# Raw weight sums behind a product's subtraction, softmax kept out of the sigmoid pairs, and a pinned gating, in a hybrid decoder step

## The chip, the cores and the metric

The kernel runs on one core of a Trainium2 chip. The core has a matrix engine (TensorE, PE in the profile), three engines for elementwise work (VectorE or DVE, ScalarE or ACT, GpSimd or POOL), a queue engine that here only issues transfers (SyncE or SP), and 16 DMA engines. Each engine works through its own list of instructions in order; an instruction that waits holds up all that stand behind it on the same engine. The metric is the device time of one execution in microseconds (us), as the median of several runs.

## The reference

One layer of a decoder with two parallel branches, stick-breaking attention and a gated short convolution, for a prompt of 512 tokens with 16 meta tokens ahead of it and for 8 sequences that each decode 4 tokens against 512 cached ones. Everything is float32.

```python
def mixer_layer(x, conv_hist, attend, g_pre, w_in, b_sb, b_gate, w_conv, b_conv, w_pa, w_pc, w_out, g_post):
    h = rmsnorm(x, g_pre)
    q, k, v, ga, cb, cc, ch, gc, ma, mc = jnp.split(h @ w_in, split_offsets(), axis=-1)
    ...
    a = attend(q, k, v, b_sb).reshape(bsz, t, D_ATTN) * jax.nn.silu(ga)
    u = cc * ch
    u_ext = jnp.concatenate([conv_hist.astype(u.dtype), u], axis=1)
    c = cb * causal_conv(u_ext, w_conv, b_conv) * jax.nn.silu(gc)
    merged = (jax.nn.sigmoid(ma + b_gate[:D_MODEL]) * (a @ w_pa)
              + jax.nn.sigmoid(mc + b_gate[D_MODEL:]) * (c @ w_pc))
    y = x + rmsnorm(merged @ w_out, g_post)
    return y, k, v, u_ext[:, -(CONV_WIDTH - 1):]
```

D_MODEL is 2048, the attention and the convolution have 1024 channels each (8 heads of 128), ma and mc 2048 each. The attention weight of a key is `sigmoid(z)` times the product of `1 - sigmoid(z)` over the keys between it and the query, computed in log space.

## The kernel before, in words

**Precision.** Every float32 operand of a large product is split in two parts, high and low, and a product is three matmuls: high x high, high x low, low x high. Weights come as raw tiles of 128 x 1024 (`w_load`, tile `raw`, one DMA each on SP's queue); `w_split` makes the high part on ACT (`whi`, L240) and the low part on DVE (`wlo`, L241). PE cannot start a product before its `whi`, nor its last third of matmuls before `wlo`.

**Seven products for eight.** For ga, cb, cc, ch, gc, ma and mc, `pair` computes two column blocks at once. It cuts the tokens into two halves and the 2048 rows of weights into two halves; that is a 2 x 2 block product, which `seven` does with seven block products in the place of eight (Strassen in Winograd's form). Each `product` is 24 matmuls (L971). The weights of the seven are `w11`, four sums and differences, `w12` and `w22`. The sums are made on DVE: `w21 + w22` (L983), that plus `w11` (L986), `w21 + w11` in place (L994), and another (L1000). L983 and L994 add raw tiles only, so they can run as soon as the DMAs have landed; both are wanted by products later in the pair. Results collect in PSUM banks: `x` and `q` from one pool (tile `mm`), `y` from another (tile `o`). In the middle of a pair, L997 subtracts a saved part from `y` to give the block (1, 1); only after that may PE write the next product into `y`. L1002 gives the block (0, 1) in the same way from `q`. The caller uses each block as it is yielded: with Silu (ga, gc), a multiplication (L1052 to L1057, L1070, L1073: the convolution) or Sigmoid on ACT (ma, mc: L1118).

**The stages.** The head of the kernel normalizes the tokens and makes q, k and v; four heads of the prompt are attended at once (`head_now`; all this takes 365 us). Then come the pairs: ga (4 pairs, tile `sg`), the convolution (4 times CC, CH, GC, CB), and the gates ma and mc (16 pairs, tile `g`). The gates are written to a scratch tensor in HBM. The pairs run from 365 to 1170 us. Then `w_pc` is applied, one group of columns at a time (L256; each group's result is multiplied with the gate `gt` read back from scratch, L1208), the four later heads are attended, and the attention outputs are multiplied by silu(ga) (`gated`, L1161). For the four early heads, both `at` and `sg` come back by DMA from scratch. At the end come `w_pa` and `w_out`.

**Decoding beside it.** `decode_steps` is a generator whose pieces are set between the products. It computes logits against the cached keys on DVE (1024 dot products, L781, each of two rows in the listings below; `kpage` and `qb` are loaded by POOL's queue), then the log-space softmax on ACT and DVE (L467 to L470 by `softplus_acts`, and L840 and L842), and then the product with the cached values (`vpage`).

**What sets the order.** Within each engine a scheduler decides it, from dependencies and from its own estimates. The kernel has two means against it. `pin`, which is `tc.keep_in_program_order`, keeps an instruction in its place relative to the other pinned ones. `tc.issue_after(ins)`, used by the change, has the instructions issued inside it come behind `ins` in the order. ACT holds one table of functions at a time; where the next function needs another, an ACT_TABLE_LOAD is inserted (Sigmoid on one side, Exp and Ln on the other). `preload_act_table_set(LNEXP)` places such a load by hand.

Of the kernel before, what the change touches and what calls it, by code (L numbers as in the profile page):

```python
# [2 lines left out]

# [57 lines left out]
def hybrid_step_kernel(  # L61
# [404 lines left out]
    def softplus_acts(e, l, r, src, bias, pin=lambda ins: ins):  # L466
        pin(act.activation(e, src, AF.Abs, bias=bias))  # L467
        pin(act.activation(e, e, AF.Exp, scale=-1.0))
        pin(act.activation(l, e, AF.Ln, bias=one_c[:e.shape[0]]))
        pin(act.activation(r, src, AF.Relu, bias=bias))  # L470

    def softplus_sums(e, l, r, t):
        dve.tensor_scalar(out=t, in0=e, scalar1=1.0, scalar2=-1.0, op0=ALU.add, op1=ALU.add)
        dve.tensor_sub(t, e, t)
        dve.tensor_add(r, r, l)
        dve.tensor_add(r, r, t)

    def softplus_parts(e, l, r, t, src, bias, pin=lambda ins: ins):

        softplus_acts(e, l, r, src, bias, pin)  # L480
        softplus_sums(e, l, r, t)


    d3ctx, hlctx, hctx, nctx = (ExitStack() for _ in range(4))
# [274 lines left out]
    def decode_steps():  # L759
# [45 lines left out]
        with tc.tile_pool(name="dec2", bufs=1, side="right") as d2:  # L805
            def tl(name, n=1):
                return d2.tile([P, n * BHT], F32, name=name)

            e, l, r, t = tl("de", 4), tl("dl", 4), tl("dr", 4), tl("dt", 4)
            S = tl("dS")  # L810
            dve.tensor_copy(S.rearrange("p (b h t) -> p b h t", b=DB, h=H),
                            bsb.unsqueeze(1).unsqueeze(3).broadcast_to([P, DB, H, DT]))
            for pg in range(NPG):
                dve.tensor_add(flat(z_all[:, pg]), flat(z_all[:, pg]), S)

            dve.memset(S, 0.0)
            rn = S[:TS]
            for p0 in (2, 0):
                pin(act.preload_act_table_set(LNEXP))
                if p0:  # L820
                    softplus_parts(e[:TS, :BHT], l[:TS, :BHT], rn, t[:TS, :BHT], zn, zero_c[:TS], pin)
                    mask_new(rn)
                c = slice(p0 * BHT, (p0 + 2) * BHT)
                softplus_parts(e[:, c], l[:, c], r[:, c], t[:, c], zf[:, c], zero_c, pin)
                if p0:
                    pn = z_ps()[:TS, :BHT]
                    pe.matmul(pn, lhsT=neg_u.bitcast(F32)[:TS, :TS], rhs=rn, start=True, stop=True)
                    dve.tensor_add(zn, pn, zn)

                for pg in (p0 + 1, p0):  # L830
                    rp = r[:, pg * BHT:(pg + 1) * BHT]
                    pz = z_ps()[:, :BHT]
                    pe.matmul(pz, lhsT=neg_u.bitcast(F32), rhs=rp, start=True, stop=False)
                    pe.matmul(pz, lhsT=neg_one.bitcast(F32), rhs=S, start=False, stop=True)
                    dve.tensor_add(flat(z_all[:, pg]), pz, flat(z_all[:, pg]))
                    if pg > 0:
                        dve.tensor_add(S, S, rp)
                yield
            pin(act.preload_act_table_set(LNEXP))
            pin(act.activation(zn, zn, AF.Exp))  # L840
            mask_new(zn)
            pin(act.activation(zf, zf, AF.Exp))  # L842
        yield "weights"

        d3 = d3ctx.enter_context(tc.tile_pool(name="dec3", bufs=1, side="right"))
# [3 lines left out]
        for g in range(2):  # L849
            for hf in range(2):  # L850
                cs = slice(hf * 512, (hf + 1) * 512)
                po = t_ps()

                def pages(vts, last):
                    for n, (lhs, rhs, pg, j) in enumerate(vts):
                        pin(pe.matmul(po[32 * j:32 * (j + 1), :], lhsT=lhs, rhs=rhs, start=(pg == 0),  # L856
                                      stop=last and n >= len(vts) - 4, tile_position=(0, 32 * j), skip_group_check=True))

                for pp in range(0, NPG, 2):
                    vts = []  # L860
                    for pg in (pp, pp + 1):
                        for j in range(4):
                            vt = d3.tile([P, 512], F32, name="vpage", bufs=9)
                            page_load(vt, vc, 4 * g + j, pg, cs)
                            vts.insert(0, (A_all[:, pg, 4 * g + j].rearrange("p h t -> p (h t)"), vt, pp, j))
                    if g + hf + pp == 0:
                        yield "values"
                    if pp == 0:
                        vts[4:] = [(l, r, 1, j) for l, r, _, j in vts[4:]]
                    else:  # L870
                        vts += [(An[:, 4 * g + j, :], vflat[:, cs], NPG, j) for j in reversed(range(4))]
                    pages(vts, pp > 0)
                    if pp == 0:
                        yield
                ob = d3.tile([P, 512], F32, name="ob")
                act.copy(ob, po)
                pt = t_ps()
                for hh in range(4):
                    pe.transpose(out=pt[:, hh * P:(hh + 1) * P], in_=ob[:, hh * P:(hh + 1) * P], identity=ident)
                for hh in range(4):  # L880
                    h = 4 * hf + hh
                    src = pt[:, hh * P:(hh + 1) * P].rearrange("p (j h t) -> p j h t", h=H, t=DT)[:, :, h, :]
                    ss = slice(16 * g, 16 * (g + 1))
                    dve.tensor_mul(sg_s[:, h, ss].rearrange("p (j t) -> p j t", t=DT), src,
                                   sg_s[:, h, ss].rearrange("p (j t) -> p j t", t=DT))
                yield

    dec = decode_steps()
    dec_at = set()
# [73 lines left out]
    def gate_bias(j, w):  # L963
        return bg[:, KD * w + j:KD * w + j + 1]

    def product(o, w, rhs, start, stop):
        hi, lo = w
        for k in range(8):
            rh, rl = rhs(k)
            for m, (l, r) in enumerate(((hi, rh), (hi, rl), (lo, rh))):  # L970
                pe.matmul(o, lhsT=l[:, k, :], rhs=r, start=(start and k == 0 and m == 0),  # L971
                          stop=(stop and k == 7 and m == 2), skip_group_check=True)

    def seven(ws, n, rb, rt, s, tmp, sums=None):

        w11, w21, w22, w12 = ws
        sums = sums or (lambda m: tmp("c"))  # L980
        x, q, y = mm_ps()[:, :n], mm_ps()[:, :n], o_ps()[:, :n]
        product(x, w_split(w11), rb(0, 0), True, False)
        dve.tensor_add(s, w21, w22)  # L983
        product(q, w_split(s), rb(0, 1), True, False)
        act.activation(y, x, AF.Copy, scale=-1.0)
        dve.tensor_add(s, s, w11)  # L986
        product(y, w_split(s), rt(0), False, False)
        s5 = tmp("s5")
        act.copy(s5, q)
        product(x, w_split(w12), rb(1, 0), False, True)  # L990
        s2 = tmp("s2")
        act.copy(s2, y)
        yield 0, 0, x
        dve.tensor_add(w21, w21, w11)  # L994
        product(y, w_split(w21), rt(1), False, False)
        c22 = sums(1)
        dve.tensor_sub(c22, y, s5)  # L997
        yield 1, 1, c22
        dve.tensor_add(s, s, w12)
        product(q, w_split(s), rb(1, 1), False, True)  # L1000
        c12 = sums(0)
        dve.tensor_sub(c12, q, s2)  # L1002
        yield 0, 1, c12
        product(y, w_split(w22), rt(2), False, True)
        yield 1, 0, y
# [28 lines left out]
    def by_query(m, half):  # L1034
        return slice(half * HQ, (half + 1) * HQ)
# [78 lines left out]
    for j in range(0, KD, 2):  # L1114
        for w, c in ((0, COL_MA), (1, COL_MC)):
            gs = [q_tile("g") for _ in range(2)]
            for m, half, b in pair(c + j * P, HQ):
                act.activation(gs[m][:, by_query(m, half)], b, AF.Sigmoid, bias=gate_bias(j + m, w))  # L1118
            if j + 2 * w == KD:
                tc.keep_in_program_order(act.preload_act_table_set(LNEXP))  # L1120
            for m in range(2):
                gate_out(j + m, w, gs[m])
            dec_group()
            if j + w == 14:

                after = hl[0].tile([P, P], F32, name="after")
                dve.tensor_scalar_add(after, neg_u.bitcast(F32), 1.0)
                loaded = head_loads(NOW, hl[0])
# [27 lines left out]
            nc.sync.dma_start(cr[:, i, :], c_scr[k + i])  # L1156
            split_evac(c_hl[:, k + i, :], c_hl[:, 8 + k + i, :], cr[:, i, :], cr[:, i, :])

    def gated(h, x, sg):

        dve.tensor_mul(sg, x, sg)  # L1161
        split_evac(a_hl[:, h, 0:PQ], a_hl[:, 8 + h, 0:PQ], sg, sg)

    def gate_load(h):
# [34 lines left out]
    for j in range(KD):  # L1199
        if j in HERE:  # L1200
            h = HERE[j]
# [12 lines left out]
        if j - 2 in HERE:  # L1214
            k = HERE[j - 2] - NOW
            sg, at = sgs.pop(k)
            gated(k, at, sg)
    split_evac(a_hl[:, 0:8, PQ:TQ], a_hl[:, 8:16, PQ:TQ], sg_s, sg_s)
    hlctx.close()
    dctx.close()  # L1220
# [51 lines left out]
    with tc.tile_pool(name="outp", bufs=1) as op:  # L1272
# [88 lines left out]
        for j in range(0, KD - 2, 2):  # L1361
# [4 lines left out]
            def tmp(name):  # L1366
                return op.tile([P, HQ], F32, name=name)
# [130 lines left out]
```

## Time and profile before

| what | value |
|---|---|
| three runs | 1580.3, 1583.6 and 1583.96 us; median 1583.6 |
| the profiled execution | 1584.74 us |
| its span, first to last instruction | 1583.1 us |
| mean granted clock of TensorE | 0.994 |
| casts `whi<-raw` / `whi<-s`, L240 | 247 and 126, 1051 and 1048 ns each |
| low parts `wlo<-raw` / `wlo<-s`, L241 | 247 and 126, 1222 and 1224 ns each |
| dot products L781 | 1024, 246.0 us of busy time |
| DMA | 252.77 MB, a mean of 160 GB/s |

The rows that follow in the text are of four kinds. A row of the page's chain gives shares of the span. A row of the view of waits reads: who waits, for whom, then the total in us, the number of waits and the longest. A row of the timeline reads: start in us from the start of the span, duration, engine, line, instruction, tile written and tiles read, sizes; in brackets at its end, how long the engine stood still ahead of it and what released it. A row of the windows gives a stretch, its length, the busy time of each engine with the number of instructions (PE, weight loads, DVE, ACT, POOL), the granted clock, the share of DMA and the GB/s.

### The profile page before, as it was taken

How to read it: one execution, taken by the hardware profiler on the slowest of the kernel's cores; microseconds unless marked ns; L12 is line 12 of the kernel's file. 1: busy time of each engine (PE TensorE's matmuls, PEld its weight loads, DVE VectorE, ACT ScalarE, POOL GpSimd, SP SyncE). 2: the span in 40 equal slices, each digit the busy share in tenths (PEclk: the TensorE clock that was granted, in tenths of full speed). 3: DMA queues.
4: the chain of work that ended last, by engine and by line, in shares of the span. 5: the costliest groups of instructions: out<-in, count | busy, mean ns of one | idle time of the engine just before them, and what ended most of it. 6: DMA issues, size and time to landing. Idle time of an engine off the chain costs nothing.

```text
span 1583.1 us, 32334 instructions
## 1 busy us (share of the span) xinstructions
PE 1560.7 (99%) x12172; PEld 1527.5 (96%) x12172; DVE 1268.5 (80%) x3574; ACT 761.7 (48%) x1345; POOL 234.7 (15%) x428
## 2 busy tenths in 40 slices
PE   8999999999999999999999999999999999999997
PEld 7999999999999999999999999898899999999997
DVE  7329999956799999999999997565678857877776
ACT  6245555435444444444444457444476734345552
POOL 1123333222111010011011102312100010000000
PEclk9999999999999999999999999999999999999999
DMA  8245556344454544445465545767595455433345
GB/s 263 82 137 186 168 160 184 107 130 136 150 180 124 151 130 140 146 134 162 120 181 173 162 138 168 245 194 226 157 306 172 148 178 165 152 107 94 101 143 183
DMA packets 300674, 252.77 MB, mean 160 GB/s; under 512 B 11521, under 2 KB 268613, under 8 KB 299701
## 3 DMA queue, kind: packets, MB, share of 16 engines
q1 hardware_dynamic: 272021, 160.45, 35.1%
q0 software_dynamic: 28368, 89.98, 17.0%
q8 instruction: 95, 1.56, 0.4%
q14 instruction: 62, 0.51, 0.1%
q10 hardware_dynamic: 128, 0.27, 0.1%
HBM read 217.95 MB, written 32.71 MB: 158 GB/s over the span
## 4 chain that ended last, share of the span: by engine, by line
PE 94%; DVE 2%; ACT 1%; DMA 1%; issue 1%; DVEq 0%; SPq 0%; ACTq 0%
PE mm L971 32%; PE mm L256 27%; PE o L971 24%; PE mm L321 2%; PE z L702 1%; PE o L714 1%; PE z L321 1%; PE tp L856 1%; DMA raw<-in_w_in 1%; PE z L620 1%; PE z L1439 1%; PE tp L505 0%; PE z L1293 0%; DVE wlo L241 0%; DMA at<-a_scr 0%
## 5 line engine op out<-in xcount | busy, mean ns | idle before, releaser
L240 ACT CAST whi<-raw 128x1024 fp32r<-128x1024 f32 x247 | 259.4, 1051 | 375.5 <-PE mm L971 135.0
L241 DVE TENSOR_TENSOR wlo<-raw,whi 128x1024 fp32r<-128x1024 f32 x247 | 301.7, 1222 | 90.2 <-ACT whi L240 88.0
L971 PE MATMUL mm<-h_hi,whi 128*128 128x272 f32 (+1 forms) x1152 | 333.5, 289 | 0.7 <-ACT whi L240 0.7
L971 PE MATMUL mm<-h_hi,wlo 128*128 128x272 f32 (+1 forms) x1152 | 332.6, 290 | 0.0
L971 PE MATMUL mm<-h_lo,whi 128*128 128x272 f32 (+1 forms) x1152 | 332.5, 289 | 0.0
L971 PE MATMUL o<-t_hi,whi 128*128 128x272 f32 (+1 forms) x864 | 251.6, 291 | 3.3 <-DVE c L997 3.3
L971 PE MATMUL o<-t_lo,whi 128*128 128x272 f32 (+1 forms) x864 | 251.2, 291 | 0.0
L971 PE MATMUL o<-t_hi,wlo 128*128 128x272 f32 (+1 forms) x864 | 251.1, 291 | 0.0
L781 DVE CUSTOM_DVE_ANT_0 junk<-kpage,qb 128x128 f32<-128x128 f32 x1024 | 246.0, 287 | 4.0 <-DMA qb<-q_scr 3.7
L971 PEld LDWEIGHTS mm<-h_hi,whi 128*128 128x128 f32 x1152 | 217.4, 189 | 6.1 <-ACT whi L240 3.5
L971 PEld LDWEIGHTS mm<-h_lo,whi 128*128 128x128 f32 x1152 | 216.8, 188 | 0.9 <-issue 0.8
L971 PEld LDWEIGHTS mm<-h_hi,wlo 128*128 128x128 f32 x1152 | 217.0, 189 | 0.2
L240 ACT CAST whi<-s 128x1024 fp32r<-128x1024 f32 x126 | 132.0, 1048 | 151.2 <-PE mm L971 48.5
L241 DVE TENSOR_TENSOR wlo<-s,whi 128x1024 fp32r<-128x1024 f32 x126 | 154.2, 1224 | 62.8 <-ACT whi L240 61.3
L256 PE MATMUL mm<-h_lo,whi 128*128 128x280 f32 (+1 forms) x640 | 187.6, 293 | 0.0
L256 PE MATMUL mm<-h_hi,wlo 128*128 128x280 f32 (+1 forms) x640 | 187.1, 293 | 0.0
L256 PE MATMUL mm<-h_hi,whi 128*128 128x280 f32 (+1 forms) x640 | 186.7, 292 | 0.0
L971 PEld LDWEIGHTS o<-t_hi,whi 128*128 128x128 f32 x864 | 164.1, 190 | 4.0 <-DVE c L997 4.0
L971 PEld LDWEIGHTS o<-t_hi,wlo 128*128 128x128 f32 x864 | 164.5, 190 | 0.9 <-issue 0.8
L971 PEld LDWEIGHTS o<-t_lo,whi 128*128 128x128 f32 x864 | 164.8, 191 | 0.0
L256 PEld LDWEIGHTS mm<-h_lo,whi 128*128 128x128 f32 x640 | 120.3, 188 | 0.8
L256 PEld LDWEIGHTS mm<-h_hi,wlo 128*128 128x128 f32 x640 | 120.5, 188 | 0.5
(452 smaller groups left out, 3166.7 us busy)
## 6 DMA issues: line engine op xcount, KB each, us to landing
raw<-in_w_in SPq DMA_DIRECT2D x192, 512.0 KB, 4.5
kpage<-in_cache_k POOLq DMA_DIRECT2D x64, 256.0 KB, 3.8
qb<-q_scr POOLq DMA_DIRECT2D x32, 512.0 KB, 5.7
vpage<-in_cache_v POOLq DMA_DIRECT2D x64, 256.0 KB, 5.7
raw<-in_w_out SPq DMA_DIRECT2D x32, 512.0 KB, 4.0
gate_scr<-g POOLq DMA_DIRECT2D x32, 272.0 KB, 4.9
gt<-gate_scr POOLq DMA_DIRECT2D x16, 544.0 KB, 4.5
raw<-in_w_pc SPq DMA_DIRECT2D x16, 512.0 KB, 4.7
```

What stands on the lines that cost most here:

```text
L240: act.copy(hi, x)
L241: dve.tensor_sub(lo, x, hi.bitcast(F32))
L256: pe.matmul(o, lhsT=w, rhs=r[:, t0:t1], start=(k == 0 and n == 0), stop=(k == nk - 1 and n == 2))
L321: pin(pe.matmul(o, lhsT=l, rhs=r[:, k, t0:t1], start=(start and m == 0), stop=(stop and m == 2), skip_group_check=True))
L620: pe.matmul(zt[:m, c0:c0 + n], lhsT=l[:, s0:s0 + m], rhs=r[:, ts:ts + n], start=(c0 == 0 and i == 0), stop=(i == 2), skip_group_check=True)
L702: pe.matmul(o, lhsT=l, rhs=x, start=False, stop=(i == len(ops) - 1), skip_group_check=True)
L714: pe.matmul(ot[:, ts - NMETA:ts - NMETA + n], lhsT=l[:m, st, :], rhs=x[:m, c0:c0 + n], start=False, stop=(g == GROUPS[-1] and i == 2), ski ...
L781: dve.tensor_tensor_reduce(out=junk, in0=kt[:, h * P:(h + 1) * P], in1=qt[:, t, h * P:(h + 1) * P], scale=1.0, scalar=0.0, op0=ALU.mult, o ...
L856: pin(pe.matmul(po[32 * j:32 * (j + 1), :], lhsT=lhs, rhs=rhs, start=(pg == 0), stop=last and n >= len(vts) - 4, tile_position=(0, 32 * j) ...
L971: pe.matmul(o, lhsT=l[:, k, :], rhs=r, start=(start and k == 0 and m == 0), stop=(stop and k == 7 and m == 2), skip_group_check=True)
L1439: pin(pe.matmul(o, lhsT=(m1, m2)[h][:, k + 8 * (q == 1), ts], rhs=two[h][q == 2][:, :, k, :], start=(n == 0), stop=(n == 47)))
```

## The change

It has three parts, and adds no arithmetic.

1. In `seven`, each pair remembers its L997 subtraction in `block_22`; the raw sums L983 and L994 of the next pair are issued behind it. Before, nothing ordered them against the pair ahead. The first pair has none ahead.
2. The softmax of the decode steps and the sigmoids of the gates are ordered against each other. Each softmax group begins with `behind_gates`: its table load comes behind the last four sigmoids issued. Each sigmoid comes behind the last activation of the softmax that the program has issued (`dec_act`).
3. `gated` takes a `pin`. For the four early heads the multiplication is kept in program order with the other pinned instructions.

```diff
     def seven(ws, n, rb, rt, s, tmp, sums=None):
+        def behind(ins):
+            return tc.issue_after(ins.ins) if ins is not None else nullcontext()
         w11, w21, w22, w12 = ws
+        last = block_22[0]
...
-        dve.tensor_add(s, w21, w22)
+        with behind(last):
+            dve.tensor_add(s, w21, w22)
...
-        dve.tensor_add(w21, w21, w11)
+        with behind(last):
+            dve.tensor_add(w21, w21, w11)
         product(y, w_split(w21), rt(1), False, False)
         c22 = sums(1)
-        dve.tensor_sub(c22, y, s5)
+        block_22[0] = dve.tensor_sub(c22, y, s5)
...
+    gate_acts, dec_act = [], [None]
+    def behind_gates():
+        with ExitStack() as stack:
+            for ins in gate_acts[-4:]:
+                stack.enter_context(tc.issue_after(ins.ins))
+            pin(act.preload_act_table_set(LNEXP))
...
             for p0 in (2, 0):
-                pin(act.preload_act_table_set(LNEXP))
                 if p0:
+                    behind_gates()
...
-                softplus_parts(e[:, c], l[:, c], r[:, c], t[:, c], zf[:, c], zero_c, pin)
+                dec_act[0] = softplus_parts(e[:, c], l[:, c], r[:, c], t[:, c], zf[:, c], zero_c, pin)
...
-            pin(act.preload_act_table_set(LNEXP))
+            behind_gates()
             pin(act.activation(zn, zn, AF.Exp))
             mask_new(zn)
-            pin(act.activation(zf, zf, AF.Exp))
+            dec_act[0] = pin(act.activation(zf, zf, AF.Exp))
...
-                act.activation(gs[m][:, by_query(m, half)], b, AF.Sigmoid, bias=gate_bias(j + m, w))
+                with tc.issue_after(dec_act[0].ins) if dec_act[0] is not None else nullcontext():
+                    gate_acts.append(act.activation(gs[m][:, by_query(m, half)], b, AF.Sigmoid,
+                                                    bias=gate_bias(j + m, w)))
...
-    def gated(h, x, sg):
-        dve.tensor_mul(sg, x, sg)
+    def gated(h, x, sg, pin=lambda ins: ins):
+        pin(dve.tensor_mul(sg, x, sg))
...
-            gated(k, at, sg)
+            gated(k, at, sg, pin)
```

Line numbers move: L781 becomes L782, L983 L1000, L986 L1003, L994 L1012, L997 L1015, L1002 L1020, L1052 L1070, L1070 L1088, L1073 L1091, L1118 L1137, L1161 L1181, L1208 L1228. A table load that the compiler inserts has the line of the activation behind it; those placed by hand had L819 and L839 and now have L896.

What the order of the engines makes of it shows at three places. The first is DVE in a pair of ga, around 425 us of the profile. `s` is the tile of weight sums, `raw` a raw weight tile, `c` the block that a subtraction gives, `o` the bank of `y`; the rows of L781 are the decode dot products. The order before, with the repeats of L781 left out:

```order
L983 TENSOR_TENSOR s<-raw 128x1024
L781 ISA junk,z_all<-kpage,qb 128x128
L781 ISA z_all 128x1
L241 TENSOR_TENSOR wlo<-raw,whi 128x1024
L994 TENSOR_TENSOR raw<-raw 128x1024
L997 TENSOR_TENSOR c<-o,s_6026 128x272
```

And now:

```order
L241 TENSOR_TENSOR wlo<-raw,whi 128x1024
L782 ISA junk,z_all<-kpage,qb 128x128
L782 ISA z_all 128x1
L1015 TENSOR_TENSOR c<-o,s_6026 128x272
L1000 TENSOR_TENSOR s<-raw 128x1024
L1124 COPY sg_s<-sg 128x32
L1012 TENSOR_TENSOR raw<-raw 128x1024
```

The two raw sums of the next pair, L983 and L994, stood ahead of the subtraction L997; they now stand behind it (L1000 and L1012 behind L1015). Five pairs of L782 stand between that `wlo` and the subtraction.

The second place is DVE in the convolution, from the (1, 1) subtraction of a CH pair to the GC pair behind it, around 493 to 503 us. `u` is the convolution's input, `cv` a tile of the convolution, `wcv` its weights, `mm` the bank of `q`. Before, with the rows of L781, L1055 to L1057 and one more `wlo<-s` left out:

```order
L997 TENSOR_TENSOR c<-o,s_6934 128x274
L241 TENSOR_TENSOR wlo<-raw,whi 128x1024
L1002 TENSOR_TENSOR c<-mm,s_6964 128x274
L986 TENSOR_TENSOR s<-s,raw 128x1024
L1052 TENSOR_TENSOR u<-o,cv 128x272
L1070 TENSOR_SCALAR cv<-u,wcv 128x512 x2
L1070 TENSOR_SCALAR cv<-u,wcv 128x32 x2
L241 TENSOR_TENSOR wlo<-s,whi 128x1024
L1073 SCALAR_TENSOR_TENSOR cv<-u,wcv,cv 128x512
```

And now, with the same rows left out:

```order
L1015 TENSOR_TENSOR c<-o,s_6934 128x274
L1000 TENSOR_TENSOR s<-raw 128x1024
L241 TENSOR_TENSOR wlo<-raw,whi 128x1024
L1012 TENSOR_TENSOR raw<-raw 128x1024
L1020 TENSOR_TENSOR c<-mm,s_6964 128x274
L1070 TENSOR_TENSOR u<-o,cv 128x272
L1003 TENSOR_TENSOR s<-s,raw 128x1024
L1088 TENSOR_SCALAR cv<-u,wcv 128x512 x2
L1088 TENSOR_SCALAR cv<-u,wcv 128x32 x2
L1091 SCALAR_TENSOR_TENSOR cv<-u,wcv,cv 128x512
L241 TENSOR_TENSOR wlo<-s,whi 128x1024
```

Between the subtraction and the last `wlo<-s` there now stand the two raw sums, one L1091 that stood behind that `wlo`, and ten pairs of L782 where there were nine of L781. All four GC pairs have this piece.

The third place is ACT around 958 to 967 us, in a pair of gate columns. `g` is the gate, `bg` its bias; `de`, `dl`, `dr` and `z_new` are tiles of the softmax. Before:

```order
L1118 ACT_TABLE_LOAD
L1118 ACTIVATE g<-mm,bg 128x272
L468 ACT_TABLE_LOAD
L468 ACTIVATE de<-de 128x512
L840 ACTIVATE z_new<-z_new 32x256
L469 ACT_TABLE_LOAD
L469 ACTIVATE dl<-de,one_c 128x512
L470 ACTIVATE dr<-z_all,zero_c 128x512
L240 CAST whi<-raw 128x1024
L1118 ACT_TABLE_LOAD
L1118 ACTIVATE g<-c,bg 128x272
```

And now, from the end of a softmax group to the start of the next:

```order
L470 ACTIVATE dr<-z_all,zero_c 128x512
L1137 ACT_TABLE_LOAD
L1137 ACTIVATE g<-mm,bg 128x272
L240 CAST whi<-raw 128x1024
L1137 ACTIVATE g<-c,bg 128x272
L240 CAST whi<-s 128x1024
L1137 ACTIVATE g<-o,bg 128x272
L1137 ACTIVATE g<-c,bg 128x272
L896 ACT_TABLE_LOAD
```

The four sigmoids of a pair now share one table load, with no softmax between them. Over the program there are nine table loads where there were fifteen.

The gating of the first early head (L1161, near 1176 us) stood in DVE's order ahead of all gate products L1208 of w_pc; six of these now stand ahead of it (L1181 behind six L1228). On SP's queue the loads of `at` and `sg` move behind the loads of gates that they stood ahead of, and the loads of a later head (`kr`, `qr`, `vn`) stand five raw weight tiles earlier; on POOL's queue a few writes of gates and of `sg` change places with loads of `qb`.

More of the change, by code (lines that the diff above doesn't have):

```diff
@@ L1 @@
-from contextlib import ExitStack
+from contextlib import ExitStack, nullcontext
 from itertools import cycle
@@ L469, in softplus_acts @@
         pin(act.activation(l, e, AF.Ln, bias=one_c[:e.shape[0]]))
-        pin(act.activation(r, src, AF.Relu, bias=bias))
+        return pin(act.activation(r, src, AF.Relu, bias=bias))
     def softplus_sums(e, l, r, t):
@@ L478, in softplus_parts @@
     def softplus_parts(e, l, r, t, src, bias, pin=lambda ins: ins):
-        softplus_acts(e, l, r, src, bias, pin)
+        last = softplus_acts(e, l, r, src, bias, pin)
         softplus_sums(e, l, r, t)
+        return last
     d3ctx, hlctx, hctx, nctx = (ExitStack() for _ in range(4))
@@ L972, in product @@
                           stop=(stop and k == 7 and m == 2), skip_group_check=True)
+    block_22 = [None]
     def seven(ws, n, rb, rt, s, tmp, sums=None):
+        def behind(ins):
+            return tc.issue_after(ins.ins) if ins is not None else nullcontext()
         w11, w21, w22, w12 = ws
+        last = block_22[0]
         sums = sums or (lambda m: tmp("c"))
```

## The prediction

> **What bounds the kernel now.** I read the page first: the busy shares, then the chain that ended last.
>
> ```profile
> span 1583.1 us, 32334 instructions
> PE 1560.7 (99%) x12172; PEld 1527.5 (96%) x12172; DVE 1268.5 (80%) x3574; ACT 761.7 (48%) x1345; POOL 234.7 (15%) x428
> PE 94%; DVE 2%; ACT 1%; DMA 1%; issue 1%; DVEq 0%; SPq 0%; ACTq 0%
> ```
>
> TensorE is busy for 1560.7 of 1583.1 us and is 94% of the chain. The change removes no matmul, so all it can win is time in which PE stands still or runs slowly, and all it can lose is a new wait of PE. So the second view is who PE waits for:
>
> ```profile
> PE o L971 <- DVE c L997: 3.3, 3, 1.8
> PE mm L256 <- DVE gt L1208: 1.7, 1, 1.7
> PE mm L971 <- ACT whi L240: 1.3, 2, 0.7
> ```
>
> Three waits for the (1, 1) subtraction L997, one for a gate product of w_pc, one in the w_in stage for a weight cast. The timeline of PE gives their size from start to start:
>
> ```profile
> 426.59 0.29 PE L971 MATMUL mm<-h_hi,whi 128*128 128x272 f32 x1
> 426.71 0.29 PE L971 MATMUL mm<-h_lo,whi 128*128 128x272 f32 x1
> 428.76 0.39 PE L971 MATMUL o<-t_hi,whi 128*128 128x272 f32 x1 [1.76 <-DVE c L997]
> 428.99 0.29 PE L971 MATMUL o<-t_lo,whi 128*128 128x272 f32 x1
> ...
> 707.10 0.28 PE L971 MATMUL mm<-h_lo,whi 128*128 128x274 f32 x1
> 708.21 0.39 PE L971 MATMUL o<-t_hi,whi 128*128 128x272 f32 x1 [0.82 <-DVE c L997]
> ...
> 965.27 0.29 PE L971 MATMUL mm<-h_hi,wlo 128*128 128x272 f32 x1
> 966.29 0.39 PE L971 MATMUL mm<-h_hi,whi 128*128 128x272 f32 x1 [0.73 <-ACT whi L240]
> 966.52 0.29 PE L971 MATMUL mm<-h_lo,whi 128*128 128x272 f32 x1
> 967.57 0.39 PE L971 MATMUL o<-t_hi,whi 128*128 128x272 f32 x1 [0.76 <-DVE c L997]
> ...
> 1175.92 0.29 PE L256 MATMUL mm<-c_hl,wlo 128*128 128x272 f32 x1
> 1177.91 0.52 PE L256 MATMUL mm<-c_hl,whi 128*128 128x272 f32 x2 [1.70 <-DVE gt L1208]
> ```
>
> Undisturbed, matmuls follow each other after 0.12 to 0.13 us (426.59 to 426.71). The five gaps lose 2.05, 1.11, 1.02, 1.05 and 1.99 us less 0.13 each, **6.6 us**, and the first matmul behind a gap takes 0.23 (428.76 to 428.99) in place of 0.13: 0.5 us for five. The windows of 4 us add what the clock does after them (columns: stretch, length, PE busy, granted clock, DMA share, GB/s):
>
> ```profile
> 428.00:432.00 4.00, 3.24 (x17) 0.69 0.48 140
> 432.00:436.00 4.00, 4.00 (x30) 0.88 0.34 100
> ...
> 968.00:972.00 4.00, 4.00 (x23) 0.60 0.00 0
> 972.00:976.00 4.00, 4.00 (x28) 0.97 0.47 154
> ...
> 708.00:712.00 4.00, 3.79 (x30) 1.00 0.36 106
> ...
> 1176.00:1180.00 4.00, 2.30 (x18) 1.00 0.88 276
> ```
>
> After the gap at 426.7, and after the two that follow each other at 965 to 967.5, the granted clock is short by 4 x (0.31 + 0.12) = 1.7 and 4 x (0.40 + 0.03) = 1.7 us: **3.4 us** together, less the two slow restarts already counted, 3.3. After 0.82 us alone, and after the 1.70, the clock stays at 1.00. In all 6.6 + 0.5 + 3.3 = **10.4 us** hang on these five gaps.
>
> **Step 1: raw sums behind L997.** No instruction is added, and the new order is one of issue only, so no engine gets a new semaphore to wait for; what changes is who stands ahead in DVE's queue. At 426.7:
>
> ```profile
> 424.01 1.23 DVE L983 TENSOR_TENSOR s<-raw 128x1024 f32<-128x1024 f32 x1 [1.21 <-DMA raw<-in_w_in]
> ...
> 426.72 1.22 DVE L994 TENSOR_TENSOR raw<-raw 128x1024 f32<-128x1024 f32 x1
> ...
> 428.27 0.43 DVE L997 TENSOR_TENSOR c<-o,s 128x272 f32<-128x272 f32 x1
> ```
>
> L997 frees the PSUM bank that PE's next product needs, and stood behind a wait for a DMA (1.21) and two sums that nobody needs yet (1.13 each at DVE's pace): 3.5 us. In the new order about five more pairs of L781 come first, of 0.21 us each. L997 then starts at 428.27 - 3.5 + 1.1 = 425.9 and ends at 426.3, while PE wants it at 426.84. The gap goes, with 0.5 us to spare. The gap at 707 has the same cause (its L983 waited longer, and the two sums stood ahead as well), and the second half of the one at 966 too. L983 now waits behind L997; its result is wanted two products later, some 6 us of PE work, so it is late for nobody where DVE has room.
>
> **Where DVE has no room** this takes something back. In the convolution's GC pair, four times:
>
> ```profile
> 480.00:520.00 40.00, 40.00 (x319) 39.95 (x318) 39.19 (x119) 16.39 (x30) 5.17 (x9) 1.00 0.49 140
> 488.25 3.08 PE o L971 x24
> ...
> 491.13 1.22 DVE L994 TENSOR_TENSOR raw<-raw 128x1024 f32<-128x1024 f32 x1
> 492.69 0.44 DVE L997 TENSOR_TENSOR c<-o,s 128x274 f32<-128x274 f32 x1
> ...
> 501.37 1.22 DVE L241 TENSOR_TENSOR wlo<-s,whi 128x1024 fp32r<-128x1024 f32 x1
> 502.72 0.74 DVE L1073 SCALAR_TENSOR_TENSOR cv<-u,wcv,cv 128x512 f32<-128x512 f32 x1
> 503.38 1.22 DVE L241 TENSOR_TENSOR wlo<-raw,whi 128x1024 fp32r<-128x1024 f32 x1
> ...
> 503.67 0.29 PE L971 MATMUL o<-t_hi,wlo 128*128 128x272 f32 x1
> ```
>
> DVE is busy 39.19 of 40 us (the third of the busy times). The wlo at 501.37 is the low half for the product that PE reaches at 503.67; it ends at 502.59, 1.1 us early. From L997 to it go 501.37 - 492.69 = 8.7 us of unbroken work. In the new order the two sums (2.26), one L1073 (503.38 - 502.72 = 0.66) and one more pair of L781 (0.21) stand between: 11.8. Against that L997 can start as soon as PE's product is out, 488.25 + 3.08 = 491.33. Then wlo starts at 503.2 and ends at 504.4: PE waits about 0.8, and with the handover I take 0.9, and 0.1 for the restart: **1.0 us, four times, 4.0**. Bounds of one: nothing, if DVE catches up; and, if L997 doesn't move forward at all, 492.69 + 11.8 + 1.2 = 505.7, a wait of 2.1. I take 0.9 because it follows from the row that frees L997. At 0.9 the clock should hold, as it did at 707.
>
> **Step 2: softmax not between sigmoids.**
>
> ```profile
> 960.42 1.28 ACT L468 ACT_TABLE_LOAD   x1
> ...
> 962.67 1.28 ACT L469 ACT_TABLE_LOAD   x1
> ...
> 965.21 1.03 ACT L240 CAST whi<-raw 128x1024 fp32r<-128x1024 f32 x1
> 966.25 1.28 ACT L1118 ACT_TABLE_LOAD   x1
> ```
>
> The cast at 965.21 is the one that PE waited for, and it stood behind loads of tables. The new order has nine loads instead of fifteen, 6 x 1.28 = 7.7 us less of ACT, and none between that pair's sigmoids. ACT as a whole is idle half the time, so the saving counts only where PE waited: the 0.89 at 965 (its 0.92 partner is step 1's), with their clock. In exchange both softmax groups stand in front of a pair's first sigmoid: a sigmoid late there would hold a bank, at worst as much as now, 0.9; at best nothing. I take nothing, since seven products, some 21 us of PE (24 matmuls in 3.08 each), cover the group. POOL's v loads are still released by the last softmax matmul and stand as many products ahead of their use as now.
>
> **Step 3: the gating.**
>
> ```profile
> 1176.21 0.69 DVE L1161 TENSOR_TENSOR sg<-at,sg 128x512 f32<-128x512 f32 x1 [2.79 <-DMA at<-a_scr]
> ```
>
> This multiplication waited 2.79 us for a load with w_pc's gate products L1208 behind it, and PE waited for those. Pinned, it stands six L1208 later, and its load and that of sg move back on SP's queue, behind the gates' loads; the DMA has landed by then and the 1.99 go. The bound on the other side is that PE waits for the next in DVE's queue, a split of 0.7 us.
>
> **Sum**, from the profiled execution's 1584.74: 1584.74 - 10.4 + 4.0 = **1578.3 us**. The median, 1583.6, lies 1.1 lower; I leave the forecast there, since whether a gap trips the clock varies from run to run and the change removes that part. What a measurement tells from no change is 0.3%, 4.75 us: below 1578.85 counts as faster.
>
> **Rivals.** (a) *The convolution's cover holds:* no new waits, 1584.74 - 10.4 = 1574.3. For it: L781 work is not urgent. Against: the new order puts it ahead of wlo, and DVE keeps its order. (b) *The change doesn't do what it says at the DVE gaps:* whatever is late (DMAs for raw, page loads) blocks DVE elsewhere, the gaps at 426, 707 and 1176 only move, and just the 966 one goes: 1.8 + 0.2 + 1.7 = 3.7 won, 4.0 lost, 1585.0. For it: L983 still waits for its DMA in the same queue. (c) *The slow stretches aren't of the gaps' making* and stay: 1578.3 + 3.3 = 1581.6. Against: they start right behind the two longest idle stretches; for: 1.70 us at 1176 made none. [...] (d) *Slower:* the GC pair's wait gets long enough to trip the clock. It decides above some 1.8 us within 3 (965 to 967.5 did it, 0.82 did not); at the upper bound each pair costs 2.1 + 0.1 + 1.7 = 3.9, four 15.6: 1584.74 - 10.4 + 15.6 = 1589.9. It needs L997 as late as now with both sums behind it, against the row at 488.25.
>
> **How the numbers follow.** Forecast 0.52 (its own range 1576 to 1580, three fifths of it below 1578.85), (a) 0.17, (b) 0.16, (c) 0.08, (d) 0.07. Faster: 0.31 + 0.17 = 0.48. Within: 0.21 + 0.16 + 0.08 = 0.45. Slower 0.07. The range takes in all but (d): 1573.5 to 1585.0.
>
> **What would show it.** Right: PE's waits no longer name L997 or L1208; the clock's windows hold 1.00 from 40 us to the end; four waits of PE near 504, 590, 675 and 761 for DVE wlo L241, 0.8 to 1.1 each; no ACT_TABLE_LOAD between the sigmoids of a pair. Wrong: such waits at more pairs than these four, a wait of PE for a sigmoid or a v page between 925 and 1000, or a lower clock behind the GC pairs.

## The result, and the profile after

| | before | after |
|---|---|---|
| median of 7 runs | 1582.13 us (1580.30 to 1585.57) | 1577.59 us (1577.47 to 1579.05) |
| ratio, 95% interval | | 0.9971 [0.9959, 0.9982] |
| profiled execution | 1584.74 us | 1577.97 us |

The kernel became 0.29% faster, 4.5 us at the medians; 1578.3 was predicted. Since 0.3% was taken as the bound, this counts as no change, by a hair; the interval excludes 1.

The page of the changed kernel gives, in the rows shown of before (span, busy shares, chain):

```profile
span 1576.4 us, 32335 instructions
PE 1557.6 (99%) x12172; PEld 1524.5 (97%) x12172; DVE 1262.8 (80%) x3574; ACT 753.0 (48%) x1339; POOL 235.5 (15%) x428
PE 94%; DVE 4%; issue 1%; ACT 1%; DVEq 0%; ACTq 0%
```

The view of waits, for PE at the products of w_in and w_pc, has only two rows left (total, number, longest):

```profile
PE o L981 <- DVE wlo L241: 2.0, 4, 0.5
PE mm L981 <- ACT whi L240: 0.7, 2, 0.5
```

No row names the subtraction (now L1015) or the gate product (now L1228). In their place are four waits for `wlo` where the prediction had them; the view counts half a microsecond of standing still for each. The longest of the second row is a cast of the w_out stage (near 1396 us) that is as long before the change. The windows of 4 us at the places of the old gaps (the granted clock is the third number from the end):

```profile
424.00:428.00 4.00, 4.00 (x35) 4.00 (x34) 4.00 (x18) 1.85 (x3) 0.00 (x0) 1.00 0.63 187
428.00:432.00 4.00, 4.00 (x34) 4.00 (x33) 4.00 (x9) 1.32 (x3) 0.24 (x1) 1.00 0.05 16
964.00:968.00 4.00, 4.00 (x34) 4.00 (x33) 4.00 (x5) 2.03 (x4) 0.00 (x0) 1.00 0.97 309
968.00:972.00 4.00, 4.00 (x37) 3.55 (x39) 2.79 (x3) 1.54 (x2) 1.09 (x2) 1.00 0.73 242
1172.00:1176.00 4.00, 4.00 (x34) 4.00 (x33) 4.00 (x11) 3.90 (x8) 0.18 (x1) 1.00 0.95 271
```

PE is busy throughout, at a granted clock of 1.00. The new wait in the first GC pair, from the timeline of DVE and then of PE:

```profile
488.84 1.22 DVE L1000 TENSOR_TENSOR s<-raw 128x1024 f32<-128x1024 f32 x1
...
492.02 1.22 DVE L1012 TENSOR_TENSOR raw<-raw 128x1024 f32<-128x1024 f32 x1
...
500.09 1.23 DVE L241 TENSOR_TENSOR wlo<-s,whi 128x1024 fp32r<-128x1024 f32 x1
```

```profile
500.60 0.27 PE L1097 MATMUL tp<-ident,lt 128*18 128x128 f32 x1
501.38 0.39 PE L981 MATMUL o<-t_hi,wlo 128*128 128x272 f32 x1 [0.50 <-DVE wlo L241]
501.61 0.29 PE L981 MATMUL o<-t_hi,whi 128*128 128x272 f32 x1
```

The two raw sums now stand ahead of this `wlo`. It starts at 500.09, which is 503.17 on before's clock (all of this stage lies 3.08 us earlier); 503.2 was worked out. PE's product starts at 501.38, or 504.46 on before's clock, in place of 503.67: 0.8 us late, and the slow restart (0.23 to the next matmul) adds 0.1.

Where did the time go? Both programs have the same matmuls of weights, in the same order but for neighbours that change places, so their starts can be compared between the two traces. Just behind the first gap the changed kernel is 3.54 us ahead; near 436 it gives back 0.46 (a cast that comes late, the other wait of the second row); over the four GC pairs it gives back 3.2; at the gap of 707 it gains 1.1; between 763 and 1015 (the stretch of the softmax) 4.1; at 1176 it gains 2.0. The last matmul is 6.9 us ahead.

### The profile page after: what moved, and what is told of

The parts are those of the page before. It is cut to its first block, busy times and chain, and to the rows that moved or that the text cites. A ratio compares the mean times of both kernels' runs of the same rounds, so it can differ in the third digit from the quotient of the medians.

```text
span 1576.4 us, 32335 instructions
## 1 busy us (share of the span) xinstructions
PE 1557.6 (99%) x12172; PEld 1524.5 (97%) x12172; DVE 1262.8 (80%) x3574; ACT 753.0 (48%) x1339; POOL 235.5 (15%) x428
## 4 chain that ended last, share of the span: by engine, by line
PE 94%; DVE 4%; issue 1%; ACT 1%; DVEq 0%; ACTq 0%
PE mm L981 31%; PE mm L256 28%; PE o L981 24%; PE mm L321 2%; PE z L703 1%; PE o L715 1%; PE z L321 1%; PE tp L857 1%; DVE wlo L241 1%; PE z L621 1%; DVE junk L782 1%; PE z L1459 1%; PE tp L506 0%; PE z L1313 0%; DVE cv L1088 0%
## 5 line engine op out<-in xcount | busy, mean ns | idle before, releaser
L782 DVE CUSTOM_DVE_ANT_0 junk<-kpage,qb 128x128 f32<-128x128 f32 x1024 | 247.0, 292 | 2.8 <-DMA qb<-q_scr 2.3
```

The costliest lines, as they stand in the source:

```text
L782: dve.tensor_tensor_reduce(out=junk, in0=kt[:, h * P:(h + 1) * P], in1=qt[:, t, h * P:(h + 1) * P], scale=1.0, scalar=0.0, op0=ALU.mult, o ...
```

## The experiments

Ratios are to the kernel before, measured on the same chip beside each run, with 95% intervals. Profiled executions differ by up to 3.7 us in their start, ahead of all that the change touches. One window of the changed kernel and the same of e9_no_pin (below), where PE had 35 matmuls and 16:

```profile
20.00:24.00 4.00, 4.00 (x35) 4.00 (x36) 4.00 (x6) 3.94 (x6) 0.71 (x2) 1.00 0.98 220
```

```profile
20.00:24.00 4.00, 3.47 (x16) 2.92 (x16) 4.00 (x7) 3.17 (x5) 0.00 (x0) 1.00 0.92 224
```

In the second the weight products start 3.46 us later, and all that follows comes later with them. The profiled executions of before and of the changed kernel start alike. So traces are compared behind the start.

| run | median, us | ratio |
|---|---|---|
| e1_sums_only (part 1 alone) | 1589.96 | 1.0043 [1.0027, 1.0059] |
| e2_softmax_only (part 2 alone) | 1593.28 | 1.0064 [1.0044, 1.0084] |
| e3_gating_only (part 3 alone) | 1581.05 | 0.9990 [0.9979, 1.0001] |
| e4_not_gc (all, GC's sums free) | 1586.24 | 1.0015 [1.0004, 1.0026] |
| e5_pool_sums | 1581.68 | 0.9988 [0.9978, 0.9998] |
| e6_own_tile | 1582.45 | 0.9994 [0.9984, 1.0005] |
| e7_dve_mask | 1576.07 | 0.9952 [0.9937, 0.9968] |
| e8_change_again | 1578.32 | 0.9972 [0.9960, 0.9985] |
| e9_no_pin (parts 1 and 2) | 1580.66 | 0.9987 [0.9976, 0.9997] |

### Each part alone

Of the diff of the change, e1_sums_only has the pieces in `seven`, e2_softmax_only those with `behind_gates` and `dec_act`, e3_gating_only the two lines of `gated`.

> Only the first part: the raw sums behind the (1, 1) subtraction; softmax, sigmoids and gating as before. Theory A (the parts add up, as the prediction has them): the gaps at 427 and 707 us and the second one at 966 us go, with the slow clock behind them or at least behind 427, the four convolution waits for wlo of 0.8 us each come; 3.5 + 1.2 + 0.9 less 0.5 less 3.2, so 2 to 4 us below the kernel before; the cast at 965 still waits behind table loads, 0.9 us. Theory B (the parts hang together: the first part alone moves the softmax by several products against the sigmoids, whose table loads then stand in front of other casts): new PE waits for ACT casts between 925 and 970 us of 3 to 7 us in all, with a fall of the clock behind the longest; the time is equal to the kernel before or up to 5 us above.

> Only the second part: softmax and sigmoids ordered against each other; raw sums and gating as before. Theory A (the parts add up): the gap at 965 us goes, and if one gap alone does not trip the clock, the slow stretch at 968 too: 0.9 + 1.7, 2 to 3 us below the kernel before; the gaps for the subtraction at 427, 707 and 967 us stay. Theory B (the parts hang together: the softmax now comes earlier on PE, after product 280 where it stood after 283, while the dot products that it needs end as late as before, near 946 us): PE waits 5 to 8 us for the softmax's first matmul, and the time is 3 to 6 us above the kernel before.

> Only the third part: the gating of the early heads pinned. Theory A (the parts add up): the one gap at 1176 us goes and nothing else moves, 1.9 to 2.0 us below the kernel before. Theory B (the load of the attention output is what is late and something else waits for it): the gap moves to another row near 1180 to 1200 us, no change.

The first two went as their theory B said, and further: each is slower than the kernel before, though both together are faster. In e1_sums_only the gaps for the subtraction are gone, but ACT, in its timeline, loads a table before nearly every second activation, and the view of waits has one row for PE at w_in that is as long as two old gaps:

```profile
922.56 1.28 ACT L819 ACT_TABLE_LOAD   x1
...
924.39 1.28 ACT L1126 ACT_TABLE_LOAD   x1
...
926.23 1.28 ACT L468 ACT_TABLE_LOAD   x1
...
928.24 1.28 ACT L469 ACT_TABLE_LOAD   x1
...
930.96 1.03 ACT L240 CAST whi<-s 128x1024 fp32r<-128x1024 f32 x1
```

```profile
PE o L971 <- ACT whi L240: 4.0, 1, 4.0
```

The windows of 4 us around it have a granted clock of 0.94, 0.50 and 0.70:

```profile
928.00:932.00 4.00, 0.05 (x1) 0.00 (x0) 1.49 (x4) 3.97 (x7) 0.59 (x1) 0.94 0.10 38
932.00:936.00 4.00, 3.83 (x15) 3.51 (x16) 3.98 (x3) 3.97 (x5) 1.97 (x2) 0.50 0.00 0
936.00:940.00 4.00, 4.00 (x22) 3.34 (x21) 3.40 (x7) 3.96 (x5) 0.00 (x0) 0.70 0.62 179
```

Part 1 lets the dot products end sooner. The last one starts at 945.5 us before and at 915.8 in e1_sums_only (the view of the line L781; the same line, L782, says 916.1 in the changed kernel):

```profile
L781 DVE CUSTOM_DVE_ANT_0 junk<-kpage,qb x1024: 260/286/721, 122.0 to 945.5; 128x128 f32<-128x128 f32 x171
```

```profile
L781 DVE CUSTOM_DVE_ANT_0 junk<-kpage,qb x1024: 259/289/718, 122.2 to 915.8; 128x128 f32<-128x128 f32 x171
```

This is mostly a matter of order: in VectorE's list the last dot product stands behind 230 low parts `wlo` in the changed kernel and in e1_sums_only, behind 239 before and in e2_softmax_only. There is one `wlo` for each product, and nine products of 3.1 us make 28 us. The softmax falls into another gate pair, where without part 2 its table loads stand between the sigmoids and ahead of a cast. In e2_softmax_only it is the reverse. The scheduler sets the first softmax matmul 3 products earlier in PE's order (behind 280 products, where before it stood behind 283; behind 277 in the changed kernel), but the dot products end as late as before, so PE arrives first (3.2 us of its wait are a select on GpSimd that takes 4.07 us in place of 0.92, see the last section):

```profile
PE z L828 <- POOL dS L803: 10.3, 1, 10.3
```

Part 3 stands by itself: the gap at 1176 is gone in e3_gating_only, nothing takes its place, and in the traces it gains 2.0 us there. Its median is 1.3 us below that of the kernel before beside it, with an interval that takes in 1.

### Is the wait in the GC pairs a loss of its own?

```diff
-        last = block_22[0]
+        last = None if free else block_22[0]
...
-        for m, half, b in pair(COL_GC + i * P, HQ):
+        for m, half, b in pair(COL_GC + i * P, HQ, True):
```

> The whole change, but the raw sums of the four GC pairs are not put behind the subtraction. Theory A (the four waits near 501, 587, 673 and 759 us are a loss of their own): they go and nothing replaces them; 3.2 us below the changed kernel, so about 1574.3. Theory B (VectorE is what bounds the stretch up to the softmax, and the waits only gave it room): the waits go, but the dot products end later against PE and PE waits for the softmax between 940 and 955 us about as much, 2 to 4 us; the time is that of the changed kernel within 1 us.

The mechanism is that of theory B, at about twice its upper bound of 4 us. The four waits go, but PE then waits 7.6 us for the softmax and its clock falls to 0.50; the kernel is 7.3 us slower than the changed one between the profiled executions (8.7 between the medians, which were not taken beside each other). The timeline of PE and the windows of e4_not_gc:

```profile
951.13 1.05 PE L828 MATMUL z<-dS,neg_u 32*32 32x256 f32 x2 [7.60 <-POOL dS L803]
```

```profile
944.00:948.00 4.00, 0.00 (x0) 0.00 (x0) 4.00 (x6) 3.97 (x6) 4.00 (x1) 0.85 0.45 131
948.00:952.00 4.00, 0.87 (x2) 0.17 (x2) 1.28 (x2) 1.35 (x4) 3.54 (x3) 0.50 0.33 98
952.00:956.00 4.00, 4.00 (x13) 3.35 (x13) 2.72 (x6) 2.22 (x3) 0.60 (x2) 0.50 0.29 104
956.00:960.00 4.00, 4.00 (x27) 3.93 (x27) 0.01 (x1) 1.07 (x2) 1.78 (x2) 0.87 0.20 74
```

The windows are short by 4 x (0.15 + 0.50 + 0.50 + 0.13) = 5.1 us of clock, which is some 10 us at half speed. About 4.3 of these 10 lie in the wait, where PE has nothing to run, so about 2.9 us of the 5.1 come on top of the 7.6; less the 3.2 of the four waits that makes the 7.3. With the GC sums free the dot products end at 932 (916 in the changed kernel) and the matmul stands 3 products later. That alone would make the wait short, 7.6 - (6.87 - 0.92) = 1.7 us if the first select below took as long as the second; the timeline of GpSimd and VectorE in e4_not_gc shows what makes it long:

```profile
943.21 6.87 POOL L801 TENSOR_SCALAR_AFFINE_SELECT dS<-dS 32x256 f32<-32x256 f32 x1 [22.50 <-DVE dS L476]
...
950.15 0.92 POOL L803 TENSOR_SCALAR_AFFINE_SELECT dS<-dS 32x256 f32<-32x256 f32 x1
```

```profile
948.08 1.20 DVE L1017 TENSOR_TENSOR s<-s,raw 128x1024 f32<-128x1024 f32 x1
952.22 0.41 DVE L829 TENSOR_TENSOR z_new<-z,z_new 32x256 f32<-32x256 f32 x1 [2.94 <-PE z L828]
```

The mask of the new tokens' softplus is two affine selects on GpSimd of one shape. The second takes 0.92 us, the first 6.87. VectorE works without a pause until 949.28 (952.22 - 2.94), and the first select ends at 950.08, 0.80 later.

### Relief for VectorE, and the shared tile

e5_pool_sums keeps the change and moves four sums to GpSimd; e6_own_tile is e4_not_gc with a tile more:

```diff
-            dve.tensor_add(s, w21, w22)
+            (eng or dve).tensor_add(s, w21, w22)      # eng is pool for the GC pairs
```

```diff
-            rn = S[:TS]
+            rn = tl("dN")[:TS]
```

> The changed kernel, with the first raw weight sum (L1000) of the four GC pairs computed by GpSimd in place of VectorE; its place behind the subtraction is kept. Theory A (VectorE has no room in that stretch, and that is all): the four waits for wlo of 0.8 us go and nothing replaces them, because VectorE now has 4 x 1.13 us less to do before the softmax; 3.2 us below the changed kernel, about 1574.4. Theory B (GpSimd's sum is slow, or slows VectorE beside it): PE waits for the cast of that sum in the second product of the GC pairs, near 494 us and three times more; about equal to the changed kernel or above it. Theory C (any other order upsets the softmax): PE waits 3 to 8 us for the softmax's first matmuls near 940 to 955 us, with a fall of the clock; 1580 to 1588.

> The kernel of e4_not_gc (raw sums of the GC pairs free), with one tile more: the softplus of the new tokens gets a tile of its own, where it shared the tile that first holds the head biases and so had to wait for the last dot product. Theory A (that shared tile is what held PE for 7.8 us in e4_not_gc): the wait for L828 goes with the slow clock behind it, no new one longer than 1 us; about 12 us below e4_not_gc, so 1574 to 1575. Theory B (the dot products themselves are late there): PE waits 3 to 6 us at the next softmax matmul L834 or its neighbours, which need the dot products in any case; 1578 to 1583.

e5_pool_sums has theory B's cause at another place: the softmax stays covered and no cast waits for the sum, but VectorE loses 2.2 us beside the second sum, and the waits for `wlo` get longer. The view of waits, then the timeline of VectorE beside the second sum, which runs from 574.14 to 576.54:

```profile
PE o L981 <- DVE wlo L241: 3.4, 4, 0.9
```

```profile
574.18 2.51 DVE L782 CUSTOM_DVE_ANT_0 junk<-kpage,qb 128x128 f32<-128x128 f32 x1
576.62 0.08 DVE L782 DVE_READ_ACCUMULATOR2_ANT z_all<- 128x1 f32 x1
```

A dot product of 0.29 us takes 2.51 us beside GpSimd's sum of 2.40: VectorE lost 2.2 us there, where it was spared a sum of 1.2. PE also waits three times for a copy on ACT there (L1002, 0.7 us in all), and over the four GC pairs the run falls 3.2 us behind the changed kernel.

In e6_own_tile the shared tile was part of the cause: the wait for the softmax falls from 7.6 to 4.5 us, at L828 still and not at L834, so theory B names the wrong matmul and theory A's wait of no more than 1 us did not come about. It is GpSimd's select again:

```profile
PE z L828 <- POOL dN L803: 4.5, 1, 4.5
```

```profile
940.59 6.69 POOL L801 TENSOR_SCALAR_AFFINE_SELECT dN<-dN 32x256 f32<-32x256 f32 x1 [20.23 <-DVE dN L476]
947.35 0.92 POOL L803 TENSOR_SCALAR_AFFINE_SELECT dN<-dN 32x256 f32<-32x256 f32 x1
```

### The select taken from GpSimd, and the third part once more

e7_dve_mask is e6_own_tile with

```diff
+    pool.memset(new_ok, 1.0)
+    mask_new(new_ok.rearrange("p b t -> p (b t)"), 1)
...
-                    mask_new(rn)
+                    dve.tensor_mul(rn4, rn4, new_ok.unsqueeze(2).broadcast_to([TS, DB, H, DT]))
```

where the first two lines stand near the start of the program; `mask_new` got the number of heads as a parameter. e9_no_pin takes `pin` from the call of `gated`.

> The kernel of e6_own_tile, with the mask of the new tokens' softplus applied by VectorE (a product with a 0/1 tile made at the start) in place of GpSimd's two affine selects. In e6_own_tile PE waited 4.5 us for the first of these selects, which took 6.69 us where it takes 0.92 to 1.1 elsewhere, and ended 0.80 us after VectorE's first pause. Theory A (GpSimd's instruction is kept out while VectorE works without a pause, and nothing else is late): the wait and the slow clock behind it go, 4.5 + 3.4; about 1 us comes back at the next softmax matmul L834; 1574 to 1576, below the changed kernel. Theory B (the select is slow because GpSimd stood still for 20 us before, or what it masks is late in any case): PE waits 3 us or more at L828 or L834; 1579 or more.

> The changed kernel once more, beside the other two on the same chip: 1577 to 1579, 0.3% below the kernel before. Its range of single runs should again be narrower than that of the kernel before (in the first runs 1577.5 to 1579.1 against 1580.3 to 1585.6), if gaps of 1 to 2 us trip the clock in some runs and not in others.

> The changed kernel without its third part (the gating of the early heads is not pinned and stands again ahead of all gate products of w_pc). Theory A (the third part is worth its gap also beside the other two): a gap of 1.5 to 2 us for L1228 near 1170 to 1180 us, 1.5 to 2 us above the changed kernel. Theory B (with the loads of head 4 earlier, the attention output lands in time): no gap, equal to the changed kernel.

e7_dve_mask goes as its theory A: no row of waits names the softmax, the kernel lies 0.48% below before and its median 2.3 us below the changed kernel's on the same chip. It is the fastest version here, though its interval and that of the changed kernel overlap a little. It isn't the same order with another mask: its matmul stands 0.83 of a product (2.6 us) later in PE's order than in e6_own_tile. But the mask's product on VectorE ends at 945.71, and PE passes the old place between 945.5 and 946.2 in the same trace, so at most 0.2 us of wait would be left there. One short wait for the subtraction is back in its trace (near 428.8 us, 0.5), behind dot products that stand elsewhere in VectorE's order.

e8_change_again confirms the ratio but not the narrow range (1577.48 to 1581.48): two of its nine runs are 3 us above the median, about the size of the step in the first 24 us; those two were not profiled, but their mean granted clock, 0.997, is that of the profiled execution of e9_no_pin, which starts late. e9_no_pin has its gap back, 1.68 us from start to start less 0.13, and is 2.3 us slower than the changed kernel at the medians, 1.8 in the traces at this place; the two intervals overlap. The timeline of PE, and the multiplication on DVE behind which the gate product stands:

```profile
1174.62 0.29 PE L256 MATMUL mm<-c_hl,wlo 128*128 128x272 f32 x1
1176.43 0.51 PE L256 MATMUL mm<-c_hl,whi 128*128 128x272 f32 x2 [1.52 <-DVE gt L1228]
```

```profile
1174.73 0.69 DVE L1181 TENSOR_TENSOR sg<-at,sg 128x512 f32<-128x512 f32 x1 [2.61 <-DMA at<-a_scr]
```

## Why the prediction was right, and where it was not

**The gaps, step 1 and step 3.** Each term came out within 0.5 us. With the slow clock the gap at 427 us was put at 3.6 and measured 3.54; the one at 707 at 1.1, measured 1.1; the one at 1176 at 1.96, measured 2.0; the two at 965 to 967 at 3.6, measured 4.1 for the whole stretch. Of this last difference 0.3 is a wait for the softmax that the view of before has and the changed kernel does not, and that the prediction left out:

```profile
PE z L833 <- DVE dr L476: 0.3, 1, 0.3
```

L1015 starts at 425.85, where 425.9 was worked out. e3_gating_only (2.0) and e9_no_pin (1.8) show the third part's gain from both sides in their traces.

**The GC pairs.** The place, the cause and the count were right, the size a little high: 1.0 per pair was predicted, 0.9 is lost at the place, and 0.1 of it comes back shortly after, because the small transposition L1097 at 500.60, which stood behind this place, now lies ahead of the wait. The row that frees the subtraction was the right one to go by; the handover was counted too high by 0.1.

**Step 2 was right only in its sum.** It took the cast at 965 as one stall and the softmax as covered by "seven products", with nothing for PE to wait for. The runs show that this cover isn't a property of part 2: alone it costs PE 10.3 us at the softmax's first matmul. What covers it is part 1, with which the dot products end 29 us sooner. The prediction listed what stands behind L997 on DVE but not what this does to the end of the dot products, and its rivals had no wait of PE for the softmax, though a scheduler that moves the softmax on ACT moves its matmuls on PE too. That this wait is absent in the changed kernel was not worked out; that the term came out at nothing was luck.

**The rivals.** (a) fell: the four waits came. But removing them, as e4_not_gc did, doesn't give their time back. (b) fell: the gaps did not move on. (c) fell in the direction that counts, since the clock holds at 1.00 from 24 to 1560 us once the gaps are gone; that a gap need not trip the clock is shown by e3_gating_only, where the pair of gaps at 965 is as long as before (0.89 and 0.92 us) and the clock stays:

```profile
964.00:968.00 4.00, 2.51 (x18) 2.07 (x17) 3.91 (x6) 3.73 (x5) 0.00 (x0) 1.00 0.00 0
968.00:972.00 4.00, 4.00 (x31) 3.90 (x31) 3.97 (x6) 0.90 (x2) 1.10 (x2) 1.00 0.12 42
```

So the 3.4 us that the sum took for the clock are a price that one execution paid, the profiled one of before, and another, that of e3_gating_only, did not pay. That the price varies in this way fits the sizes: 6.4 us were predicted from the profiled execution, 6.8 lie between the profiled executions, and 4.5 between the medians. It isn't shown, since the medians also hold the differences of the start. (d) fell: at these waits of 0.8 us the clock stayed at 1.00. Its bound for a fall, 1.8 us of gaps within 3, does not hold either: e3_gating_only has these gaps and no fall. **0.46 us** near 436 was not foreseen: a cast that stands on ACT behind another, which waits for the weight sum L1003. It is a near miss, and in the profile of e8_change_again, the same kernel, PE does not wait there.

## What to carry to other kernels

Before crediting an ordering edge with the stall that it removes, follow the engine on which it makes room to the next thing that this engine feeds: here the room went to dot products, and the softmax behind them decided whether parts 1 and 2 won or lost. Parts of a change that share a scheduler can each lose alone and win together, so try them apart and together. And an edge that costs a short wait may hold something else in place: with it taken back in four pairs, four waits of half a microsecond went and one of 7.6 came.

## What the runs showed of the hardware

At places in these runs an instruction of VectorE beside one of GpSimd is longer than elsewhere: by 2.2 us beside the sum of 2.40 in e5_pool_sums, where it ends 0.15 us after that sum, and in the changed kernel the cast's low part takes 1.78 us in place of 1.22 beside a select of 1.06:

```profile
932.53 1.06 POOL L801 TENSOR_SCALAR_AFFINE_SELECT dS<-dS 32x256 f32<-32x256 f32 x1 [8.26 <-DVE dS L476]
```

```profile
932.72 1.78 DVE L241 TENSOR_TENSOR wlo<-s,whi 128x1024 fp32r<-128x1024 f32 x1
```

Three selects were long: 6.87, 6.69 and, in e2_softmax_only, 4.07 us. Each ended 0.80 to 0.81 us after the start of VectorE's first pause, which is why they are read here as kept out until then. GpSimd had also stood still for 20 to 28 us ahead of these three; that this alone makes a select slow is less likely, since the shortest of them follows the longest rest, but no run rules it out. No run shows by what one of the two engines would hold up the other. Two of the long selects, 6.87 and 6.69 us, lay beside eight and nine VectorE instructions in a row, some 6 us, which was not expected; why the select at 932.5 took 1.06 us and the one at 943.2 took 6.87 stays open.

The fall of the clock was longer around the longer wait: behind 1.76 us of standing still (before, at 427) the windows are short by 1.7 us, around 7.6 us (e4_not_gc) by 5.1, of which some 2.2 lie in the wait itself and cost nothing. Gaps of nearly one length went both ways in before: behind the 1.76 us the window shows 0.69, behind the 1.70 at 1176 it shows 1.00; what decides it was not tried.
